# A hybrid conv and retention layer: the heads' norm made chunk by chunk with tokens on partitions, and queries and rotation tables without the token's norm and decay

## The chip, the cores and the metric

One core of one Trainium2 chip runs the whole layer in one launch. The metric is the device time of an execution in microseconds (us). Engines are named as the profile names them: PE (TensorE matmul), PEld (its weight loads), DVE (VectorE), ACT (ScalarE), POOL (GpSimd), SP (SyncE, which issues the DMAs).

## The reference

All arrays are float32, with 1024 tokens of 1024 channels (`D_MODEL`), 8 chunks of 128 tokens, and 4 retention heads of 128 channels.

```python
def rms_norm(x, g, eps=1e-6):
    return x * rsqrt(mean(x * x, -1) + eps) * g

u = rms_norm(x, norm1_g)
z = u @ w_in                       # 3 x 512 conv columns, then q, k, v and gate, 512 each
y_conv = group_rms_norm(cb * causal_dwconv3(cc * ch, conv_w), conv_norm_g, 8)

q, k = rotary(rq), rotary(rk) * 128 ** -0.5
# by head and chunk of 128 tokens, gamma_h = 1 - 2 ** (-5 - h):
scores = q @ k.T * decay           # gamma ** (i - j) where i >= j, else 0
o = scores @ v + (q * xi) @ S      # xi = gamma ** (i + 1)
S = gamma ** 128 * S + (k * zeta).T @ v
y_ret = group_rms_norm(o, ret_norm_g, 4) * silu(rg)

x = x + concat(y_conv, y_ret) @ w_out
x = x + relu(rms_norm(x, norm2_g) @ w_up) ** 2 @ w_down
return rms_norm(x, final_norm_g)
```

## The kernel before, in words

Activations lie with channels on partitions and tokens along the row, so a tile `unit` is 128 channels x 1024 tokens; `hs` are its two halves of 512 tokens. A float32 product is made of three matmuls of rounded float32 parts: each operand is split into a high part (`uh`, `wh`, `U`, made by an ACT copy) and the rest (`ul`, `wl`, made by a subtraction on DVE or POOL). `mm` issues them (before, line 361; 365 in the changed file).

The kernel has these stages, each with its place in the profiled execution:

1. Values (line 323, 6 to 54 us). `v`, with tokens on partitions, is x times its weights, without the token's norm. In the second half of this stage the sum of squares `ssq` is reduced by a matmul with ones (line 333). From it come `R`, the reciprocal norm of every token, laid out along the row on all 128 partitions, and `rtok`, the same with tokens on partitions. The norm of layer input is not applied to x: it is multiplied in later, into what x was projected to.
2. Projections by `tile_in`, two matrix banks (`pm`) of 512 tokens and 48 matmuls each, in four quarters of 12 matmuls. `rot_tiles` makes two such tiles A and B, multiplies both by the cosine and sine tables `ropes` out of PSUM into `ac`, `as_`, `t2`, `t3`, and adds and subtracts these to `q[0]` and `q[1]` (64 partitions each, half on POOL, half on DVE). It runs for queries, then keys, of head pair p = 0, then 1.
3. Retention of a head pair, a generator that is resumed once a quarter, between the matmuls of the tiles of the next stage. A step takes one chunk: scores, turned keys (line 545), and for the chunk before it the product with the values (570), the product with the state (572) and the state's update (578).
4. More projections (`IN_WHOLE`), then the last ones as products of half-sized sums (`pair_in`, seven products for eight), for which `rights` reads x again (`xs`) as soon as the second pair's retention is marked as done.
5. The gate and the convolution (`conv_h`, `conv_b`, `gate`) run beside stages 3 and 4. Then come the output projection (from 375 us), the MLP and the last norm.

PE's order is that of the program. Around it, small planned tasks (`procs`) are asked at every quarter which of them may issue: `background` compares a clock per engine, made of costs per column, with the time of the matmul stream, and where an operation may run on POOL or DVE it takes the one that would end first. So a change of what the tasks issue also moves other tasks' operations from one of the two to the other. Nothing moves an instruction once it is issued: each engine works through its list.

The heads' norm is one of these tasks (`norm`, line 429): for 512 tokens of one head it squares `o` on ACT, splits the square, sums it over the partitions by two matmuls with a matrix of ones (`onesr`, lines 441 and 442), takes the square root on ACT and the reciprocal of 128x512 on DVE, and multiplies `o` by it on POOL or DVE. There are 8 of these, and 8 for the groups of the convolution (`blkr`).

Of the kernel before, what the change touches and what calls it, by code (L numbers as in the profile page):

```python
# [16 lines left out]
P = 128  # L17
# [53 lines left out]
def hybrid_layer(  # L71
# [11 lines left out]
    decay: bass.AP,  # L83
    zeta: bass.AP,
# [139 lines left out]
    onesr = xp.tile([P, P], F32R, name="onesr")  # L224
    dve.tensor_copy(onesr, ones.to_broadcast([P, P]))
# [3 lines left out]
    onesf = xp.tile([P, P], F32, name="onesf")  # L229
    dve.memset(onesf, 1.0)  # L230
# [45 lines left out]
    dec = xp.tile([P, NH, P], F32, name="dec")  # L276
    nc.sync.dma_start(dec, decay)
    zxt = xp.tile([P, NH], F32, name="zxt")
    nc.sync.dma_start(zxt, zeta)
    ropes = [unit(s="rope") for _ in range(6)]  # L280
# [31 lines left out]

    v = [unit(s="v") for _ in range(NC_ // 2)]
    rtok = cp.tile([P, NC_], F32, name="rtok")
    zr = xp.tile([P, NH, NC_], F32, name="zr")
    for half in range(2):
        vb = [bank(pr if half else pm) for _ in range(4)]
        for k in range(KT):
# [11 lines left out]
            if half == 1 and k == 3:  # L330
                for c, sl in ((0, hs[0]), (4, hs[1])):
                    b = bank(pm)
                    nc.tensor.matmul(b, onesf, ssq[:, sl], start=True, stop=True)
                    t = tmp()
                    act.activation(t, b, AF.Sqrt, bias=eps, scale=1.0 / D)
                    dve.reciprocal(R[:, sl], t)
                    t = tmp().rearrange("p (a b) -> p a b", b=P)
                    dve.tensor_mul(
                        t,
                        R[:, sl].rearrange("p (a b) -> p a b", b=P),  # L340
                        ident[:, None, :].to_broadcast([P, 4, P]),
                    )
                    dve.reduce_sum(rtok[:, c : c + 4], t, axis=mybir.AxisListType.X)
# [9 lines left out]
    prepare(2)  # L353

# [169 lines left out]
    def retention(p, q, k):  # L524

        h0 = 2 * p
        S = None
        pend = None
        o = [unit(s="o") for _ in range(2)]
        for c in range(NC_ + 1):  # L530
# [3 lines left out]
            if c < NC_:  # L534
                sl = slice(c * P, (c + 1) * P)
                bs = bank(pr)
                for j in range(2):
                    nc.tensor.matmul(  # L538
# [3 lines left out]
                if c < NC_ - 1:  # L542
                    bt = bank(pr)
                    for j in range(2):
                        nc.tensor.transpose(bt[:, j * P : (j + 1) * P], k[j][:, sl], ident)
# [861 lines left out]
```

## Time and profile before

| what | value |
|---|---|
| median of 3 runs | 1109.75 us (1109.44 to 1110.27) |
| profiled execution | 1111.85 us, of which the span of instructions is 1110.0 us |
| PE busy | 1065.7 us (96%) |
| DVE busy | 926.0 us (83%) |
| POOL busy | 578.1 us (52%) |
| ACT busy | 454.2 us (41%) |
| chain that ended last | PE 77%, DVE 14%, issue 3%, DMA 2%, ACT 2%, POOL 1% |
| mean granted clock of PE | 0.982 of full speed |

The busy share is a mean over stages that have different limits. The table of windows shows which engine is full in which stage; the chain of waits and the order of time around a place show what ends a wait there. Times in a view are microseconds from the start of the span.

### The profile page before, as it was taken

How to read it: one execution, taken by the hardware profiler on the slowest of the kernel's cores; microseconds unless marked ns; L12 is line 12 of the kernel's file. 1: busy time of each engine (PE TensorE's matmuls, PEld its weight loads, DVE VectorE, ACT ScalarE, POOL GpSimd, SP SyncE). 2: the span in 40 equal slices, each digit the busy share in tenths (PEclk: the TensorE clock that was granted, in tenths of full speed). 3: DMA queues.
4: the chain of work that ended last, by engine and by line, in shares of the span. 5: the costliest groups of instructions: out<-in, count | busy, mean ns of one | idle time of the engine just before them, and what ended most of it. 6: DMA issues, size and time to landing. Idle time of an engine off the chain costs nothing.

```text
span 1110.0 us, 13715 instructions
## 1 busy us (share of the span) xinstructions
PE 1065.7 (96%) x4872; PEld 883.4 (80%) x4872; DVE 926.0 (83%) x1171; ACT 454.2 (41%) x817; POOL 578.1 (52%) x393
## 2 busy tenths in 40 slices
PE   7999999998798799989999999999999999999997
PEld 6778888887586588867788888888888888888886
DVE  8786486689999845579999989989989899899945
ACT  8211431456236433354344343433443343434453
POOL 6253234437776323536827629448267286284553
PEclk9999999999899899989999999999999999999998
DMA  7311112130111523032131120221211201200204
GB/s 266 143 57 48 30 39 75 49 142 16 36 46 46 199 86 124 1 100 71 48 96 29 49 86 29 67 58 39 79 37 58 86 29 48 86 20 19 70 9 152
DMA packets 38868, 76.68 MB, mean 69 GB/s; under 512 B 4368, under 2 KB 6416, under 8 KB 38800
## 3 DMA queue, kind: packets, MB, share of 16 engines
q1 hardware_dynamic: 38800, 75.80, 21.1%
q8 instruction: 39, 0.64, 0.2%
q14 instruction: 29, 0.24, 0.1%
HBM read 70.02 MB, written 5.77 MB: 68 GB/s over the span
## 4 chain that ended last, share of the span: by engine, by line
PE 77%; DVE 14%; issue 3%; DMA 2%; ACT 2%; POOL 1%; SPq 0%; DVEq 0%; POOLq 0%; ACTq 0%
PE b L361 49%; PE b L1159 22%; DVE wl L65 3%; PE b L323 2%; DVE U L65 1%; DVE t L65 1%; DVE r L65 1%; DVE z L65 1%; DVE xs L65 1%; DMA wv<-w_v 1%; DVE x L65 1%; DVE cv L65 1%; POOL r L65 1%; PE b L570 1%; PE b L538 1%
## 5 line engine op out<-in xcount | busy, mean ns | idle before, releaser
L65 ACT CAST wh<-r 128x512 fp32r<-128x512 f32 x286 | 176.7, 620 | 385.0 <-PE b L361 204.0
L361 PE MATMUL b<-U,wh 128*128 128x512 f32 x992 | 310.5, 394 | 8.5 <-DVE z L65 3.6
L65 DVE TENSOR_TENSOR wl<-r,wh 128x512 fp32r<-128x512 f32 x257 | 240.2, 937 | 76.1 <-ACT wh L65 75.2
L65 POOL TENSOR_TENSOR r<-r,r 128x512 f32<-128x512 f32 x136 | 210.2, 1548 | 131.6 <-DVE wl L65 79.6
L1159 PE MATMUL b<-V,wh 128*128 128x512 f32 x784 | 242.3, 390 | 1.1 <-POOL V L65 1.1
L361 PEld LDWEIGHTS b<-U,wh 128*128 128x128 f32 x992 | 188.4, 190 | 50.2 <-issue 4.4
L65 DVE TENSOR_TENSOR x<-x,b 128x512 f32<-128x512 f32 (+1 forms) x320 | 198.1, 665 | 28.7 <-PE b L361 28.7
L361 PE MATMUL b<-U,wl 128*128 128x512 f32 x496 | 195.3, 394 | 0.0
L1159 PEld LDWEIGHTS b<-V,wh 128*128 128x128 f32 x784 | 147.0, 188 | 33.1 <-POOL V L65 1.9
L65 POOL TENSOR_TENSOR t<-t,t 128x512 f32<-128x512 f32 x70 | 106.8, 1530 | 101.5 <-ACT t L65 55.4
L1159 PE MATMUL b<-V,wl 128*128 128x512 f32 x392 | 152.5, 389 | 0.0
L361 PE MATMUL b<-uh,wh 128*128 128x512 f32 x320 | 107.0, 399 | 4.3 <-DVE z L65 4.3
L361 PEld LDWEIGHTS b<-U,wl 128*128 128x128 f32 x496 | 94.5, 191 | 19.9
L361 PE MATMUL b<-uh,wl 128*128 128x512 f32 x320 | 105.6, 395 | 1.9 <-DVE wl L65 1.9
L361 PE MATMUL b<-ul,wh 128*128 128x512 f32 x320 | 105.9, 396 | 0.7 <-DVE ul L65 0.7
L65 POOL TENSOR_TENSOR wl<-r,wh 128x512 fp32r<-128x512 f32 x29 | 39.3, 1356 | 98.2 <-ACT wh L65 92.7
L1159 PEld LDWEIGHTS b<-V,wl 128*128 128x128 f32 x392 | 73.6, 188 | 15.2
L65 POOL TENSOR_TENSOR V<-t,V 128x512 fp32r<-128x512 f32 x35 | 49.1, 1402 | 67.2 <-ACT V L65 67.2
L65 DVE TENSOR_TENSOR t<-t,b 128x512 f32<-128x512 f32 x112 | 76.1, 680 | 1.7 <-POOL t L65 1.2
L65 ACT ACTIVATE t<-t 128x512 f32<-128x512 f32 x64 | 40.3, 631 | 84.6 <-DVE t L65 83.9
L361 PEld LDWEIGHTS b<-uh,wh 128*128 128x128 f32 x320 | 60.2, 192 | 17.6 <-issue 4.5
L361 PEld LDWEIGHTS b<-uh,wl 128*128 128x128 f32 x320 | 61.0, 191 | 15.3 <-DVE wl L65 2.4
(155 smaller groups left out, 1505.1 us busy)
## 6 DMA issues: line engine op xcount, KB each, us to landing
r<-w_up_t SPq DMA_DIRECT2D x64, 256.0 KB, 2.6
r<-w_down_t SPq DMA_DIRECT2D x56, 256.0 KB, 2.6
r<-w_in_t SPq DMA_DIRECT2D x48, 256.0 KB, 2.6
xt<-xT SPq DMA_DIRECT2D x16, 256.0 KB, 5.4
xs<-xT SPq DMA_DIRECT2D x8, 512.0 KB, 6.2
r<-w_out_t SPq DMA_DIRECT2D x16, 256.0 KB, 2.6
x<-xT SPq DMA_DIRECT2D x8, 512.0 KB, 8.8
rope<-rope SPq DMA_DIRECT2D x6, 512.0 KB, 6.8
```

The costliest lines, as they stand in the source:

```text
L65: return f(out, *args, **kw)
L323: nc.tensor.matmul(vb[i], a[k][:, tsl], b[k // 2][:, vs], start=(k == 0 and a is uh and b is vh), stop=(k == KT - 1 and a is ul),)
L361: nc.tensor.matmul(b, a[:, k, :], rhs(n, k)[r], start=(start and i == 0), stop=(stop and i == len(ops) - 1),)
L538: nc.tensor.matmul(bs[:, j * P : (j + 1) * P], k[j][:, sl], q[j][:, sl], start=True, stop=True)
L570: nc.tensor.matmul(bo[:, js], vj, sc[:, js], start=True, stop=(S is None))
L1159: nc.tensor.matmul(b, a, r, start=(i == 0), stop=(i == len(ops) - 1))
```

## The change

Four things are changed together.

- `ropes` are only cosine and sine (2 tables for 6); they are not multiplied by `R` any more, and the queries' decay `xi` is not in them. Queries and keys so stay without their token's norm, and queries without their decay. What a key lacks is put in where the scores and the turned keys leave PSUM (`by_key`, `by_state`, a number per token and head, from r squared). What a query lacks is a factor of a whole row of `o`, which the heads' norm divides out; its epsilon is scaled instead (`by_query`).
- `R` and `rtok`: eight one-column matmuls give the sums with tokens on partitions; `R` is made from `rtok` by `spread_norms`, called after the first two tiles (the queries of pair 0): a broadcast copy on DVE, four 128x128 matmuls per half, a copy and a square on ACT.
- Retention gives `o` with tokens on partitions (the operands of lines 570 and 572 change places). Each step then makes the norm of its chunk: two squares on ACT out of PSUM with a sum along the row, three operations on 128x2 (DVE, ACT, DVE), two scaled copies on ACT. One step later two PE transposes and two ACT copies turn it back into `o`. Scores and turned keys now share a bank, as do `bo` and `bk`.
- The 8 norm tasks of the heads are gone, with `onesr`.

```diff
-    onesr = xp.tile([P, P], F32R, name="onesr")
-    dve.tensor_copy(onesr, ones.to_broadcast([P, P]))
...
-    ropes = [unit(s="rope") for _ in range(6)]
+    ropes = [unit(s="rope") for _ in range(2)]
...
             if half == 1 and k == 3:
-                for c, sl in ((0, hs[0]), (4, hs[1])):
-                    b = bank(pm)
-                    nc.tensor.matmul(b, onesf, ssq[:, sl], start=True, stop=True)
-                    t = tmp()
-                    act.activation(t, b, AF.Sqrt, bias=eps, scale=1.0 / D)
-                    dve.reciprocal(R[:, sl], t)
...
-                for i in (0, 1, 4, 5, 2, 3):
-                    pool.tensor_mul(ropes[i], ropes[i], R)
-                R2 = ssq
-                pool.tensor_mul(R2, R, R)
+                b = bank(pm)
+                for c in range(NC_):
+                    nc.tensor.matmul(
+                        b[:, c : c + 1], ssq[:, c * P : (c + 1) * P], ones, start=True, stop=True
+                    )
+                act.activation(ms, b[:, :NC_], AF.Identity, bias=eps, scale=1.0 / D)
+                dve.reciprocal(r2, ms)
+                act.activation(rtok, r2, AF.Sqrt)
                 for h in range(NH):
-                    dve.tensor_scalar_mul(zr[:, h, :], rtok, zxt[:, h : h + 1])
+                    for i, (to, src) in enumerate(((by_key, r2), (by_state, r2), (by_query, ms))):
+                        dve.tensor_scalar_mul(to[:, h, :], src, perhead[:, i, h : h + 1])
...
+    def spread_norms():
+
+        for half, sl in enumerate(hs):
+            r = rtok[:, 4 * half : 4 * half + 4]
+            d = tmp().rearrange("p (a b) -> p a b", b=P)
+            dve.tensor_copy(d, r[:, :, None].to_broadcast([P, 4, P]))
+            b = spread([d[:, j] for j in range(4)])
+            act.copy(R[:, sl], b)
+            act.square(R2[:, sl], R[:, sl])
...
-        for c in range(NC_ + 1):
+        for c in range(NC_ + 2):
...
                 for j in range(2):
-                    nc.tensor.matmul(bo[:, js], vj, sc[:, js], start=True, stop=(S is None))
+                    nc.tensor.matmul(bo[:, js[j]], sc[:, js[j]], vj[j], start=True, stop=(S is None))
...
-                for j in range(2):
-                    act.copy(o[j][:, psl], bo[:, j * P : (j + 1) * P])
...
-                        asked.append((o[j][:, hs[half]], onesr, 1.0 / P, done, clock[act], 0.0))
+                for j in range(2):
+                    act.activation(
+                        on[:, js[j]], bo[:, js[j]], AF.Square, accum_out=m[:, j : j + 1]
+                    )
+                dve.scalar_tensor_tensor(
+                    m, m, 1.0 / P, by_query[:, h0 : h0 + 2, pc], ALU.mult, ALU.add
+                )
+                act.activation(m, m, AF.Sqrt)
+                dve.reciprocal(m, m)
+                for j in range(2):
+                    act.activation(on[:, js[j]], bo[:, js[j]], AF.Copy, scale=m[:, j : j + 1])
+                turn = (pc, on)
+            if turned is not None:
+                pc, on = turned
+                b = bank(pr)
+                for j in range(2):
+                    nc.tensor.transpose(b[:, js[j]], on[:, js[j]], ident)
+                for j in range(2):
+                    act.copy(o[j][:, pc * P : (pc + 1) * P], b[:, js[j]])
...
     for p in range(2):
-        q = rot_tiles(ropes[2 * p], ropes[2 * p + 1])
-        k = rot_tiles(ropes[4], ropes[5])
+        q = rot_tiles(*ropes)
+        if p == 0:
+            spread_norms()
+        k = rot_tiles(*ropes)
```

What this does to the lists of the engines is shown at three places. The first is PE at the end of the first queries' tile B and the start of the keys' tile A, before the change (`uh`, `ul` and `wh`, `wl` are the parts of x and of the weights):

```order
L361 MATMUL b_615<-uh_153,wh_541 128x512
L361 MATMUL b_616<-uh_153,wh_541 128x512
L361 MATMUL b_615<-ul_161,wh_541 128x512
L361 MATMUL b_616<-ul_161,wh_541 128x512
L361 MATMUL b_615<-uh_153,wl_542 128x512
L361 MATMUL b_616<-uh_153,wl_542 128x512
L361 MATMUL b_695<-uh_146,wh_575 128x512
L361 MATMUL b_696<-uh_146,wh_575 128x512
```

The same place on PE with the change; `t_682` and `t_691` are the broadcast copies of `rtok`:

```order
L365 MATMUL b_604<-uh_149,wh_530 128x512
L365 MATMUL b_605<-uh_149,wh_530 128x512
L365 MATMUL b_604<-ul_157,wh_530 128x512
L365 MATMUL b_605<-ul_157,wh_530 128x512
L365 MATMUL b_604<-uh_149,wl_531 128x512
L365 MATMUL b_605<-uh_149,wl_531 128x512
L304 MATMUL b_684<-ident,t_682 128x128 x4
L304 MATMUL b_693<-ident,t_691 128x128 x4
L365 MATMUL b_702<-uh_142,wh_564 128x512
L365 MATMUL b_703<-uh_142,wh_564 128x512
```

Eight matmuls that read DVE's copies stand between the last matmul of the queries and the first of the keys. The second place is DVE's work that follows the queries' tile B, before (`b_615`, `b_616` are its two banks):

```order
L65 TENSOR_TENSOR t_677<-b_615,rope_281 128x512
L65 TENSOR_TENSOR t_678<-b_615,rope_280 128x512
L65 TENSOR_TENSOR q_614<-ac_545,t_677 64x512
L65 TENSOR_TENSOR q_613<-t_678,as_546 64x512
L65 TENSOR_TENSOR t_685<-b_616,rope_281 128x512
L65 TENSOR_TENSOR t_686<-b_616,rope_280 128x512
L65 TENSOR_TENSOR q_614<-ac_545,t_685 64x512
L65 TENSOR_TENSOR q_613<-t_686,as_546 64x512
L65 TENSOR_TENSOR wl_724<-r_603,wh_723 128x512
```

And DVE there with the change:

```order
L65 TENSOR_TENSOR t_666<-b_604,rope_277 128x512
L65 TENSOR_TENSOR t_667<-b_604,rope_276 128x512
L65 TENSOR_TENSOR q_603<-ac_534,t_666 64x512
L65 TENSOR_TENSOR q_602<-t_667,as_535 64x512
L65 TENSOR_TENSOR t_674<-b_605,rope_277 128x512
L65 TENSOR_TENSOR t_675<-b_605,rope_276 128x512
L65 TENSOR_TENSOR q_603<-ac_534,t_674 64x512
L65 TENSOR_TENSOR q_602<-t_675,as_535 64x512
L65 COPY t_682<-rtok 128x512
L65 COPY t_691<-rtok 128x512
L65 TENSOR_TENSOR wl_731<-r_592,wh_730 128x512
```

The two copies stand behind the eight operations that read tile B. The third place is ACT at the end of the second pair's retention, before (`b_2066` is the bank of a norm's sum, `xs` is x read again):

```order
L65 COPY o_1599<-b_1998 128x128
L65 COPY o_1600<-b_1998 128x128
L65 ACTIVATE t_2017<-o_1599 128x512
L65 CAST s_2018<-t_2017 128x512
L65 ACTIVATE t_2019<-o_1600 128x512
L65 CAST s_2020<-t_2019 128x512
L65 CAST wh_2041<-r_1766 128x512
L65 ACTIVATE r_2069<-b_2066,eps 128x512
L65 ACTIVATE xs_2005<-xs_2005,sm 128x1024
```

And ACT there with the change (`h_2095` is a normed chunk, `m_2096` its two norms, `b_2104` and `b_2142` the turned chunks):

```order
L65 ACTIVATE h_2095,m_2096<-b_2090 128x128 x2
L65 ACTIVATE m_2096<-m_2096 128x2
L65 ACTIVATE h_2095<-b_2090,m_2096 128x128 x2
L65 COPY o_1644<-b_2104 128x128
L65 COPY o_1645<-b_2104 128x128
L65 CAST wh_2135<-r_1826 128x512
L65 COPY o_1644<-b_2142 128x128
L65 COPY o_1645<-b_2142 128x128
L65 ACTIVATE xs_2109<-xs_2109,sm 128x1024
```

The squares of 128x512 and the square root that waited for a norm's matmul no longer stand ahead of `xs`.

## Rows read from the trace of the kernel before

**Rows 1.** The page: busy time and share of the span of PE.

```profile
PE 1065.7 (96%) x4872; PEld 883.4 (80%) x4872; DVE 926.0 (83%) x1171; ACT 454.2 (41%) x817; POOL 578.1 (52%) x393
```

**Rows 2.** Windows by stage: PE, PEld, DVE, ACT, POOL busy, clock, DMA share.

```profile
75.00:100.00 25.00, 25.00 (x112) 20.71 (x111) 14.22 (x18) 3.12 (x5) 5.93 (x5) 1.00 0.18 53
100.00:250.00 150.00, 150.00 (x795) 128.57 (x795) 106.77 (x123) 56.87 (x126) 58.91 (x43) 1.00 0.20 66
250.00:375.00 125.00, 104.37 (x418) 82.35 (x416) 120.98 (x111) 57.98 (x94) 87.71 (x57) 0.92 0.14 40
```

**Rows 3.** Timeline of ACT behind tile B: start, duration, operation, idle before it.

```profile
77.37 0.62 ACT L65 CAST wh<-r 128x512 fp32r<-128x512 f32 x1 [4.82 <-PE b L361]
```

**Rows 4.** Timeline of DVE behind the first queries' tile B.

```profile
78.63 1.28 DVE L65 TENSOR_TENSOR t<-b,rope 128x512 f32<-128x512 f32 x2
...
85.58 1.67 DVE L65 TENSOR_TENSOR q<-t,as 64x512 f32<-64x512 f32 x1
87.27 0.69 DVE L65 TENSOR_TENSOR wl<-r,wh 128x512 fp32r<-128x512 f32 x1
```

**Rows 5.** Timeline of DVE before the MLP: the same broadcast copy of norms.

```profile
476.02 0.43 DVE L65 COPY t<-rtok 128x512 f32<-128x512 f32 x1
```

**Rows 6.** Timeline of PE before the MLP: one-column sums (L290) and spreads (L308).

```profile
468.92 0.95 PE L290 MATMUL b<-ones,t 128*128 128x1 f32 x8
...
477.28 1.95 PE L308 MATMUL b<-ident,t 128*128 128x128 f32 x16
478.98 0.71 PE L361 MATMUL b<-U,wh 128*128 128x512 f32 x2
```

**Rows 7.** Windows around waits of PE, columns as in rows 2.

```profile
371.00:378.00 7.00, 3.04 (x7) 2.47 (x8) 6.91 (x10) 3.48 (x7) 1.64 (x1) 0.51 0.51 161
301.00:306.30 5.30, 5.30 (x13) 4.14 (x14) 3.64 (x6) 0.23 (x1) 0.00 (x0) 0.51 0.37 102
```

**Rows 8.** Timeline of PE in the first queries' tile B: a wait for DVE.

```profile
67.52 0.73 PE L361 MATMUL b<-uh,wl 128*128 128x512 f32 x2 [1.93 <-DVE wl L65]
```

**Rows 9.** Chain of waits, first 110 us: start, length, what.

```profile
41.15 1.72 PE b L333 x4
...
108.15 0.22 PE b L545 x2
```

**Rows 10.** Chain of waits at the end of the second retention.

```profile
240.03 5.46 PE b L361 x24
245.49 0.23 PE b L441
245.72 0.25 PE b L442
...
246.58 1.76 ACT xs L65 x2
...
251.37 1.60 DVE xs L65
```

**Rows 11.** Groups of DVE between 250 and 375 us: count, busy, mean ns, idle before.

```profile
L65 DVE RECIPROCAL r<-r 128x512 f32<-128x512 f32 x8 | 26.7, 3343 | 0.7 <-ACT r L65 0.7
L65 DVE TENSOR_TENSOR wl<-r,wh 128x512 fp32r<-128x512 f32 x19 | 20.5, 1081 | 0.1
...
L65 DVE TENSOR_TENSOR s<-t,s 128x512 fp32r<-128x512 f32 x4 | 4.7, 1165 | 0.0
...
L65 DVE TENSOR_TENSOR z<-z,R 128x512 f32<-128x512 f32 x1 | 1.7, 1748 | 0.0
...
L65 DVE TENSOR_TENSOR z<-z,cv 128x512 f32<-128x512 f32 x1 | 0.7, 687 | 0.0
```

**Rows 12.** Groups between 105 and 150 us: turned keys on ACT.

```profile
L65 ACT ACTIVATE h<-b,zr 128x128 f32<-128x128 f32 x14 | 4.4, 367 | 12.3 <-PE b L545 12.3
```

**Rows 13.** Timelines of DVE and POOL, 36 to 105 us: small and large operations at once.

```profile
56.02 8.60 DVE L65 TENSOR_SCALAR zr<-rtok,zxt 128x8 f32<-128x8 f32 x4
52.31 14.59 POOL L65 TENSOR_TENSOR rope<-rope,R 128x1024 f32<-128x1024 f32 x6 [19.65 <-DVE R L65]
```

More of the change, by code (lines that the diff above doesn't have):

```diff
@@ L274, in hybrid_layer @@
     prepare(2)
[L276 to L279, printed above, removed]
-    ropes = [unit(s="rope") for _ in range(6)]
+    causal = xp.tile([P, P], F32, name="causal")
+    nc.sync.dma_start(causal, mask)
+    perhead = xp.tile([P, 3, NH], F32, name="perhead")
+    nc.sync.dma_start(perhead, heads)
+    ropes = [unit(s="rope") for _ in range(2)]
     for i, t in enumerate(ropes):
@@ L314, in hybrid_layer @@
     rtok = cp.tile([P, NC_], F32, name="rtok")
-    zr = xp.tile([P, NH, NC_], F32, name="zr")
+    ms = xp.tile([P, NC_], F32, name="ms")
+    r2 = xp.tile([P, NC_], F32, name="r2")
+    by_key, by_state, by_query = (xp.tile([P, NH, NC_], F32, name=s_) for s_ in ("bk", "bz", "bq"))
     for half in range(2):
@@ L526, in retention @@
         h0 = 2 * p
-        S = None
-        pend = None
+        S = pend = turn = None
         o = [unit(s="o") for _ in range(2)]
-        for c in range(NC_ + 1):
+        js = [slice(j * P, (j + 1) * P) for j in range(2)]
+        for c in range(NC_ + 2):
             yield None
@@ new lines, in retention @@
+                act.activation(m, m, AF.Sqrt)
[8 more added lines that the diff above has]
+                    nc.tensor.transpose(b[:, js[j]], on[:, js[j]], ident)
+                for j in range(2):
+                    act.copy(o[j][:, pc * P : (pc + 1) * P], b[:, js[j]])
+                    if pc % 4 == 3:
+                        o_n[h0 + j, pc // 4] = o[j]
+                        mark(("o", h0 + j, pc // 4), act)
@@ L604, in retention @@
             retention_task[0].ready = max(clock[act], clock[dve])
-        mark(("retention", p), act)
+            if c == NC_:
+                mark(("retention", p), act)
     a_of, cvs = {}, {}
@@ L1317, in _constants @@
     cos, sin = (np.tile(f(ang), (2, 1)) for f in (np.cos, np.sin))
+    rope = np.stack([cos, sin])
     lg = np.log(1.0 - 2.0 ** (-5.0 - np.arange(NH)))
     i = np.arange(P)
-    xi = np.exp(lg[:, None] * (np.arange(T) % P + 1.0)[None])
-    xi = [np.repeat(xi[2 * p : 2 * p + 2], half, axis=0) for p in range(2)]
-    rope = np.stack([cos * xi[0], sin * xi[0], cos * xi[1], sin * xi[1], cos, sin])
+    mask = i[None, :] >= i[:, None]
     scale = P**-0.5
-    decay = np.where(
-        (i[None, :] >= i[:, None])[:, None, :],
-        np.exp(lg[None, :] * (-1.0 - i)[:, None])[:, :, None] * scale,
-        0.0,
-    )
-    zeta = np.exp(lg[None, :] * (P - 1.0 - i)[:, None]) * scale
-    return [np.ascontiguousarray(a, np.float32) for a in (rope, decay, zeta)]
+    heads = np.stack(
+        [
+            np.exp(lg[None] * (-1.0 - i)[:, None]) * scale,
+            np.exp(lg[None] * (P - 1.0 - i)[:, None]) * scale,
+            np.exp(lg[None] * -2.0 * (i + 1.0)[:, None]) * EPS,
+        ],
+        axis=1,
+    )
+    return [np.ascontiguousarray(a, np.float32) for a in (rope, mask, heads)]
 def kernel(x, norm1_g, w_in, conv_w, conv_norm_g, ret_norm_g, w_out, norm2_g, w_up, w_down,
@@ L1376 @@
     )
-    rope, decay, zeta = _constants()
+    rope, mask, heads = _constants()
     arrays = {
@@ L1390 @@
         "rope": rope,
-        "decay": decay,
-        "zeta": zeta,
+        "mask": mask,
+        "heads": heads,
     }
```

74 lines of the change are left out of this document (27 added, 47 removed).

## The prediction, made before the changed kernel was run

> **What bounds the kernel now.** I read the page first. PE is busy for 96% of the span [rows 1], so what counts is where PE stands idle, and whether its list gets longer. The windows by stage say where: from 75 to 250 us PE is never idle and the granted clock is 1.00, though DVE, ACT and POOL have room; from 250 to 375 us it is busy for only 104.4 of 125 us at a mean clock of 0.92, and DVE for 121.0 [rows 2]. So there are two regimes. In the first, through both retentions, any idle time that PE gets is lost for good, and work taken from DVE, ACT or POOL is worth nothing. In the second, DVE is the limit for most of the stretch, and DVE's work and the moment at which it starts count. The change takes work from DVE and POOL and gives some to ACT, and most of the reciprocals that it removes lie in the first regime. Then I compared the lists of the engines, since a stall in the first regime is the one thing to fear.
>
> **Part by part.**
>
> *The first stage.* The two matmuls with ones took 1.72 us of PE [rows 9]; that goes. Eight one-column sums take their place: 0.95 us [rows 6]. The reciprocals of 128x512, the tables' products on POOL and the slow small products (8.60 us for four of 128x8, beside POOL's 14.59 us [rows 13]) leave DVE before 64 us. One wait ended on them: PE stood 1.93 us for a weight part that DVE made too late [rows 8]. With all this gone from DVE and POOL, that wait goes, and I see no other behind it, since the split in question waits only for ACT's copy. Sum of the stage: -1.72 + 0.95 - 1.93 = -2.7 us.
>
> *The spread of the norm.* This is the term that decides. On PE the eight spreads stand right behind the queries' tile B, ahead of the keys' tile A. They read two copies on DVE that stand behind the eight operations which empty tile B, and the first of those needs tile B's last matmuls. In the kernel before, the keys' first matmul followed at once. When tile B ends is seen on ACT: a cast that waits for B's last weights to be free starts at 77.37 [rows 3]. DVE's eight operations ran from 78.63 to 87.27, that is 8.64 us [rows 4]; the copy takes 0.43 [rows 5]; two hand-overs between engines are put at 0.1 us each, an estimate. PE idle: 8.64 + 0.43 + 0.2 = 9.3 us. The first four spreads hide the second copy. All eight cost 1.70 us of PE (477.28 to 478.98 [rows 6]). Everything else that PE could do stands behind them in its list. The bounds of the idle time: if POOL did not hold DVE's 64-partition operations up they would take 0.69 us, as the uncontended subtraction does [rows 4], and the chain 2 x 1.28 + 4 x 0.69 + 0.6 = 5.9 us; if POOL's additional split of a weight, which now stands ahead of its part of the queries, comes between, 1.2 us more than my value (half of 14.59 / 6 [rows 13]), 10.5 us. I take 9.3, since the same eight operations run beside the same four of POOL.
>
> *The clock behind that wait.* After a wait of 6.7 us the granted clock was 0.51 from 371 to 378 us, of which PE worked 3.04; after one of 3.6 us it was 0.51 for 5.30 us of work [rows 7]. That is the lower level, 1.2 for 2.4 GHz, and half of such work is lost: 1.5 to 2.7 us. I take 2.0.
>
> *Retention on PE.* Eight norms with ones go: 0.23 + 0.25 = 0.48 us each [rows 10], -3.8 us. 32 turns come, at 0.11 us (two in 0.22 [rows 9]): +3.5 us. The operands that change places keep their size. Together -0.3 us.
>
> *Retention on ACT and DVE.* Each of the 16 chunk steps adds two squares, a root, two scaled copies, and replaces nothing else but copies; a pass over 128x128 costs ACT 4.4 / 14 = 0.31 us [rows 12], pipelined. With two passes for the keys, two squares, a root (the same 0.31 as a bound), two scaled copies and two turned copies, a step is 9 x 0.31 = 2.8 us of ACT, plus two trips to DVE and back in the middle, where no row shows a price: between the 0.1 us of a hand-over and a whole POOL operation, 1.2 us (half of 14.59 / 6 us for 1024 columns [rows 13]). A step's period on PE is 12 matmuls (half of 5.46 us [rows 10]) and 20 passes of 0.11 us, 4.9 us. So ACT is busy for 3 to 4 us of 4.9, and PE, which reads the normed chunk only in the next step, has over 2 us in hand. I cost it at nothing; the cover is that one step of distance, and without it each step would cost what is late.
>
> That the small operation on 128x2 can be held up by POOL is what the row of the small products shows: 128x8 took 2.15 us apiece while POOL multiplied tables, each as long as one of POOL's operations [rows 13]. The Trainium skill (SBUF — State Buffer, Who interferes with whom) says that VectorE and GpSimd share one pair of ports as an exclusive lock, and that an instruction with two SBUF inputs contends with a reading GpSimd one. By that rule each of the 16 would wait up to a whole POOL operation, and the sum would stay as it is, as 1.2 us is less than the time in hand; it speaks for the third rival below.
>
> *The stretch from 250 to 375 us.* Before, the re-read x came to ACT only after the norm's matmul: 24 matmuls, the norm, a root, then the first scaling at 246.58 and DVE's first difference at 251.37 [rows 10]. With the change ACT reaches it behind the last turned copy, that is after 12 matmuls, two turns and two copies: 246.58 - 240.03 = 6.55 us before, 2.73 + 0.22 + 0.5 = 3.45 now. DVE so starts 3.1 us earlier against PE. What it has to do from there on, counted in the lists up to the last operation before the output projection: one reciprocal less (3.34), four splits of weights less (4 x 1.08), one of a square less (1.2) and a small sum (0.7), together -9.5; and +4 products with R, +3 with the convolution, one difference of x and one split more, nine of 0.69 to 1.75 us, at 1.2 us each +10.8. So the planner gives back to DVE what the norms leave: +1.3 us. POOL has five operations less there, some 7 us of its 87.7 [rows 2], and as an uncontended split takes 0.69 and the mean one 1.08 [rows 4, 11], about a third of that comes back to DVE: -2.3 us. Sum: -3.1 + 1.3 - 2.3 = -4.1 us. Bounds: +4 if the nine all take 1.75 us and POOL gives nothing, -9 if they take 0.69 and DVE is the limit throughout.
>
> *Behind 375 us* the lists are the same, and PE is the limit.
>
> **Sum.** -2.7 + 9.3 + 1.7 + 2.0 - 0.3 - 4.1 = +5.9 us. On the profiled execution (span 1110.0 and 1.85 around it, 1111.85) that is 1117.8. That execution lies 2.1 above the median of the runs, 1109.75; put on the median the forecast is 1115.6 us, slower by 0.5%.
>
> **Rivals.**
>
> 1. *The stretch gives all of it back.* The wait in front of the keys is paid, but DVE, which starts with less behind it, ends the stretch 9 us or more earlier, and PE, which waits for it 20.6 us there [rows 2], follows. For it: those 20.6 us and the clock of 0.92. Against it: the count of DVE's work, which is nearly the same. -2.7 + 9.3 + 1.7 + 2.0 - 0.3 - 9 = +1 us: 1110.8.
> 2. *DVE is no longer the limit between 250 and 375 us.* This ends on the other side. One mechanism: with less of POOL in its way DVE keeps ahead of the matmuls, and PE's idle 20.6 us goes, and with it some of the 10 us that a clock of 0.92 is worth over 125 us. It decides from the point at which the stretch shrinks by more than 10 us; with 15 us the time is 1109.75 + 10 - 15 = 1104.8. Against it: the six reciprocals of the convolution stay, 20 of the 26.7 us [rows 11]. The same side comes out if the wait for the spread is not there at all (1104.3), for which nothing in the lists speaks.
> 3. *The chunk's chain is late.* Square, sum, root, reciprocal and scaling cross between ACT and DVE four times; if POOL's lock or ACT's other copies make it longer than a step, PE stands at the turns, in the regime where all is lost. At 0.5 us in each of 16 steps +8 us: 1123.6. Against it: over 2 us in hand.
>
> **How the numbers follow.** Forecast 0.62, with its own range 1112.5 to 1119; rival 1: 0.14; rival 2 and the missing wait: 0.10; rival 3: 0.14. The range 1109.5 to 1122.5 holds the forecast, rival 1 and the near half of rival 3, and leaves out rival 2 and the far half. A measurement of this kernel can tell about 0.2% (2.2 us) from no change. Slower: forecast, rival 3 and a little of rival 1, 0.78; within: most of rival 1, 0.12; faster: 0.10.
>
> **What would show it.** In the profile after: one gap of PE of 8 to 10 us at about 75 us, ended by DVE's copy at the spread, with a lower granted clock behind it; no wait in the queries' tile B; no gaps in the two retentions; DVE over 0.9 busy again in the 125 us that follow the second one, and the output projection starting some 6 us later than the 375 us of now. The forecast is wrong if that gap is under 5 us, if PE waits at the turns, or if the stretch behind the second retention is shorter by more than 9 us.

## The result, and the profile after

The changed kernel takes 1114.2 us (median of 5 runs, 1113.53 to 1115.23), the kernel before 1110.23 in the same session (5 runs, 1109.44 to 1110.35): a ratio of 1.0038, 95% interval 1.0025 to 1.0051. It is slower by 0.4%; 1115.6 had been forecast. One run of experiment 3 took 6104 us and is left out of its times below.

The profiled executions stand closer together: 1113.53 us against 1111.85 (spans 1111.7 and 1110.0). That of before lies 1.6 above the median beside it, that of after 0.7 below. So the traces have to explain +1.7, the runs +4.0, and the difference of 2.3 is between executions (experiment 12).

The page of the kernel after, its line of busy times (of before: [rows 1]):

```profile
PE 1064.8 (96%) x4916; PEld 885.2 (80%) x4916; DVE 872.1 (78%) x1207; ACT 462.1 (42%) x909; POOL 542.7 (49%) x377
```

The windows of after, with the columns of [rows 2] (PE, PEld, DVE, ACT, POOL, granted clock, DMA); the last one is the eight spreads by themselves:

```profile
75.00:100.00 25.00, 16.04 (x72) 13.53 (x72) 11.04 (x13) 4.30 (x7) 8.04 (x6) 0.80 0.08 22
100.00:250.00 150.00, 150.00 (x809) 129.12 (x808) 81.34 (x157) 58.45 (x201) 44.43 (x33) 1.00 0.21 67
250.00:375.00 125.00, 109.16 (x465) 86.32 (x464) 118.18 (x115) 62.57 (x107) 79.37 (x54) 0.98 0.14 43
...
84.39:87.82 3.43, 3.43 (x16) 3.43 (x17) 0.28 (x1) 1.21 (x2) 0.00 (x0) 0.50 0.00 0
```

DVE is busy 54 us less than before, and the kernel is slower. In the first 25 us shown PE now stands idle for 9; through the retentions it is again never idle; in the third window it works 4.8 us more than before.

The timeline of PE in after at the spread: the last matmuls of the queries' tile B, the spreads, the keys' first matmul.

```profile
74.81 0.61 PE L365 MATMUL b<-uh,wl 128*128 128x512 f32 x2
84.39 3.72 PE L304 MATMUL b<-ident,t 128*128 128x128 f32 x16 [8.96 <-DVE t L65]
87.82 0.73 PE L365 MATMUL b<-uh,wh 128*128 128x512 f32 x2
```

The timeline of DVE in after, over the same wait (of before: [rows 4]): eight operations on tile B, then the copy that PE waits for.

```profile
75.31 1.29 DVE L65 TENSOR_TENSOR t<-b,rope 128x512 f32<-128x512 f32 x2 [7.39 <-PE b L365]
76.63 0.90 DVE L65 TENSOR_TENSOR q<-ac,t 64x512 f32<-64x512 f32 x1
77.56 1.64 DVE L65 TENSOR_TENSOR q<-t,as 64x512 f32<-64x512 f32 x1
...
83.90 0.76 DVE L65 COPY t<-rtok 128x512 f32<-128x512 f32 x2
```

This is the wait that was forecast. After it the granted clock is 0.50, the lower level, and the spreads take 3.43 us.

Behind the second retention, the timelines of ACT and DVE in after where the re-read x arrives (of before: [rows 10]):

```profile
253.78 0.43 ACT L65 COPY o<-b 128x128 f32<-128x128 f32 x2
254.10 4.28 ACT L65 ACTIVATE xs<-xs,sm 128x1024 f32<-128x1024 f32 x4
```

```profile
253.33 1.29 DVE L65 TENSOR_TENSOR z<-b,R 128x512 f32<-128x512 f32 x2 [1.49 <-PE b L365]
254.54 1.17 DVE L65 TENSOR_TENSOR z<-z,cv 128x512 f32<-128x512 f32 x1
255.63 1.78 DVE L65 TENSOR_TENSOR xs<-xs 128x512 f32<-128x512 f32 x1
```

And the same spot in before, where a reciprocal of the heads' norm stood ahead of x on DVE:

```profile
246.99 3.34 DVE L65 RECIPROCAL r<-r 128x512 f32<-128x512 f32 x1
250.25 1.00 DVE L65 TENSOR_TENSOR xs<-xs 128x512 f32<-128x512 f32 x1
```

The keys' first matmul is PE's next one behind the queries' tile B; in the timeline of before it starts at 77.62:

```profile
77.62 0.62 PE L361 MATMUL b<-uh,wh 128*128 128x512 f32 x2
```

The last product of the second retention with the state ends at 240.03 in before and 250.55 in after, 162.4 and 162.7 us behind that matmul. From there DVE needs 10.2 us to get to x in before (250.25) and 5.1 in after (255.63). The output projection starts at 374.96 and 375.91: 134.9 us behind the end of that product before, 125.4 after. So the two traces add up in this way:

| piece | before to after, us |
|---|---|
| first matmul (6.31, then 5.79) | -0.5 |
| from there to the end of the queries' tile B | -1.7 |
| wait at the spread | +9.0 |
| spreads, at clock 0.50 | +3.4 |
| retentions | +0.3 |
| last product with the state to the output projection | -9.6 |
| from the output projection on | +0.8 |
| sum | +1.7 |

A delay of 12.4 us in front of the keys, and 9.6 us given back behind the retentions. The windows of that stretch, from the end of the last product with the state to the output projection, first in before, then in after:

```profile
240.03:374.96 134.93, 114.30 (x462) 90.46 (x460) 129.06 (x116) 65.25 (x105) 91.30 (x59) 0.92 0.13 39
```

```profile
250.55:375.91 125.36, 108.61 (x461) 85.80 (x459) 119.06 (x117) 63.20 (x108) 79.37 (x54) 0.98 0.15 43
```

PE's idle time falls by 3.9 us (20.6 to 16.8), the time it works by 5.7, with a mean granted clock of 0.98 for 0.92; DVE is busy for 10.0 us less. Three explanations fit the 9.6. **Theory A**: these are two independent effects; the spread costs its 12 us in any case, and the new norm saves its 9.6 in any case, so the loss can be had back without losing the gain. **Rival B**: the stretch behind the retentions, where PE waits for other engines anyway, takes up whatever delay it is given; then the norm saves little, and removing the wait gains little. **Rival C**: the higher clock gives the time back, whatever DVE does.

### The profile page after: what moved, and what is told of

Read it like the earlier page. It is cut to its first block, busy times and chain, and to the rows that moved or that the text cites. A ratio compares the mean times of both kernels' runs of the same rounds, so it can differ in the third digit from the quotient of the medians.

```text
span 1111.7 us, 13918 instructions
## 1 busy us (share of the span) xinstructions
PE 1064.8 (96%) x4916; PEld 885.2 (80%) x4916; DVE 872.1 (78%) x1207; ACT 462.1 (42%) x909; POOL 542.7 (49%) x377
## 4 chain that ended last, share of the span: by engine, by line
PE 75%; DVE 12%; issue 2%; ACT 2%; POOL 1%; DVEq 0%; POOLq 0%; ACTq 0%
PE b L365 49%; PE b L1173 22%; DVE wl L65 2%; DVE z L65 2%; DVE r L65 1%; DVE U L65 1%; DVE x L65 1%; DVE t L65 1%; PE b L571 1%; PE b L542 1%; PE b L573 1%; PE b L579 1%; DVE xs L65 1%; DVE cv L65 1%; PE b L304 1%
## 5 line engine op out<-in xcount | busy, mean ns | idle before, releaser
L65 DVE TENSOR_TENSOR wl<-r,wh 128x512 fp32r<-128x512 f32 x249 | 227.5, 916 | 112.2 <-ACT wh L65 111.4
L65 POOL TENSOR_TENSOR r<-r,r 128x512 f32<-128x512 f32 x136 | 207.9, 1531 | 131.2 <-DVE wl L65 79.5
L65 POOL TENSOR_TENSOR wl<-r,wh 128x512 fp32r<-128x512 f32 x37 | 49.8, 1350 | 166.4 <-ACT wh L65 150.3
L365 PEld LDWEIGHTS b<-ul,wh 128*128 128x128 f32 x320 | 60.3, 189 | 15.7 <-DVE ul L65 2.9
```

The source lines that it names most:

```text
L65: return f(out, *args, **kw)
L365: nc.tensor.matmul(b, a[:, k, :], rhs(n, k)[r], start=(start and i == 0), stop=(stop and i == len(ops) - 1),)
```

## The experiments

Experiments 1 to 4, 5 to 8, and 9 to 11 each share their runs of before (medians 1110.42, 1109.88 and 1110.08 us). Where kernels of different groups are compared below, their ratios to before give the same differences within 0.4 us.

**1. The spread moved up.** The copies follow the small products on DVE, the spreads follow the values on PE; behind that all lists are as in the changed kernel.

```diff
+    spread_norms()            # right behind the values' loop, banks from pm
     prepare(2)
...
         q = rot_tiles(*ropes)
-        if p == 0:
-            spread_norms()
```

> The changed kernel with the spread of the tokens' norm moved: its copies stand on DVE behind the small products at 45 us, its matmuls on PE right behind the values' matmuls at 53.5 us. Behind that the lists of all engines are those of the changed kernel. Theory A (PE's wait of 8.97 us at the spread and the lower clock behind it are a loss by themselves, and the retention's new norm saves its share whether they are there or not): the wait goes and the spreads take 1.7 instead of 3.43 us, 1114.2 - 8.97 - 1.7 = 1103.5 us, and the output projection starts some 10.7 us before 375.9. Rival B (the stretch behind the second retention takes up whatever PE lost before it, since PE waits there for other engines anyway): that stretch gets longer by most of 10 us, the output projection starts at 374 to 375 us as in both kernels, 1112 to 1114 us.

Measured: 1102.79 us (1102.59 to 1104.12; 0.9935 of before, 0.9924 to 0.9947). The timeline of PE: no wait, and half the time for the spreads.

```profile
53.90 1.95 PE L304 MATMUL b<-ident,t 128*128 128x128 f32 x16
55.60 0.71 PE L366 MATMUL b<-uh,wh 128*128 128x512 f32 x2
...
365.49 0.77 PE L366 MATMUL b<-yh,wh 128*128 128x512 f32 x1 [6.06 <-ACT z L65]
```

53.90 to 55.60 is 1.70 us for the same eight spreads, at a granted clock of 1.00. The output projection starts 10.4 us earlier than in after: the wait and the clock are pure loss, and nothing of the norm's gain depends on them. A held, B did not.

**2. The kernel before with the same spreads, of no use.**

```diff
         q = rot_tiles(ropes[2 * p], ropes[2 * p + 1])
+        if p == 0:
+            for half in range(2):
+                r = rtok[:, 4 * half : 4 * half + 4]
+                d = tmp().rearrange("p (a b) -> p a b", b=P)
+                dve.tensor_copy(d, r[:, :, None].to_broadcast([P, 4, P]))
+                b = spread([d[:, j] for j in range(4)])
+                t = tmp()
+                act.copy(t, b)
+                act.square(t, t)
         k = rot_tiles(ropes[4], ropes[5])
```

> The kernel before, with two broadcast copies of the tokens' norm on DVE behind the first queries' tile B, eight spreads on PE ahead of the keys' tile A and two copies and squares on ACT, whose results nobody uses; all else as it was. Theory A: PE loses the wait (9 to 10 us), the spreads (1.7) and the clock (1.7), nothing is given back, 1110.2 + 12.5 = 1122.7 us. Rival B (the stretch takes the delay up by itself): the output projection starts at 375 to 378 us instead of 375, 1111 to 1114 us. Between the two, what is given back without the new norm is read from the stretch.

Measured: 1124.39 us (1124.22 to 1124.93; 1.0129, 1.0116 to 1.0142), +14.0; between the traced spans it is 12.4 (1122.4 and 1110.0). The timeline of PE at the spread and at the output projection:

```profile
85.17 3.78 PE L308 MATMUL b<-ident,t 128*128 128x128 f32 x16 [9.88 <-DVE t L65]
88.60 1.20 PE L361 MATMUL b<-uh,wh 128*128 128x512 f32 x2
...
386.42 0.76 PE L361 MATMUL b<-yh,wh 128*128 128x512 f32 x1 [6.64 <-DVE z L65]
```

From the keys' first matmul to the output projection are 297.8 us; in before they are 297.3 (77.62 to 374.96). So with the old norm the delay is not given back: the stretch moves as a whole. The same trace decides Rival C. The window of the stretch:

```profile
252.41:386.42 134.01, 109.52 (x461) 86.17 (x460) 129.46 (x116) 65.23 (x105) 91.29 (x59) 0.98 0.13 40
```

PE has the clock of 0.98 here, and works 4.8 us less than in before; but it then waits 24.5 us for 20.6, and the stretch is only 0.9 us shorter. What stayed is DVE's work, 129.5 us for 129.1. C did not hold.

**3 and 9. The new norm alone.** Retention as in after, first stage as in before (two tables with the token's norm, no spread).

```diff
-                b = bank(pm)
-                for c in range(NC_):
-                    nc.tensor.matmul(
-                        b[:, c : c + 1], ssq[:, c * P : (c + 1) * P], ones, start=True, stop=True
...
+                    nc.tensor.matmul(b, onesf, ssq[:, sl], start=True, stop=True)
...
+                for i in range(2):
+                    pool.tensor_mul(ropes[i], ropes[i], R)
```

> The retention of the changed kernel (norm with tokens on partitions, turned back), with the first stage of the kernel before: matmuls with ones of 128x512, wide reciprocals, POOL multiplies two tables with the tokens' norm, no spread. Theory A: the norm saves what the changed kernel gave back, so 1110.2 - 7 = 1103 us, with the output projection starting some 6 to 7 us before 375. Rival B: without a delay to take up the stretch has nothing to give, 1109 to 1110 us. The prediction's own term for it (-0.3 on PE, -4.1 in the stretch) gives 1105.8.

Measured: 1100.92 us (median of five runs, 1100.59 to 1102.68; 0.9922, 0.991 to 0.9934), 9.5 below the median of before, 8.7 by the ratio. The trace is that of experiment 9, the same kernel.

> The kernel with the new norm alone once more, for its trace: time 1101.8 us as before; a wait of some 1.9 us in the first queries' tile B, none at the keys; from the keys' first matmul to the output projection 288 us as in the changed kernel, where the kernel before had 297.6.

Measured: 1101.52 us (one run). The output projection starts at 363.76, 287.8 us behind the keys' first matmul (the queries' first, 54.20, and 96 matmuls of 0.2267); in after it is 288.1 (87.82 to 375.91). The expected wait in tile B was not there: PE has no wait of over 0.6 us between its first matmul and 264 us. Why is seen on DVE and POOL:

```profile
56.99 1.53 DVE L65 TENSOR_SCALAR bk<-rtok,perhead 128x8 f32<-128x8 f32 x1
58.44 1.94 DVE L65 TENSOR_SCALAR bz<-rtok,perhead 128x8 f32<-128x8 f32 x1
60.29 1.33 DVE L65 TENSOR_SCALAR bq<-ones,perhead 128x8 f32<-128x8 f32 x1
61.53 0.22 DVE L65 TENSOR_SCALAR bk<-rtok,perhead 128x8 f32<-128x8 f32 x1
```

```profile
53.28 5.21 POOL L65 TENSOR_TENSOR rope<-rope,R 128x1024 f32<-128x1024 f32 x2 [20.07 <-DVE R L65]
58.46 1.89 POOL L65 TENSOR_TENSOR ssq<-R 128x1024 f32<-128x1024 f32 x1
60.31 1.28 POOL L65 TENSOR_TENSOR wl<-r,wh 128x512 fp32r<-128x512 f32 x1
```

A product of 128x8 takes 0.22 us alone and 1.3 to 1.9 as long as POOL is at work. With two tables instead of six POOL is done at 61.6, and DVE's first weight split comes in time.

**4. The new first stage and the spread alone**, with the retention of before.

```diff
-        q = rot_tiles(ropes[2 * p], ropes[2 * p + 1])
-        k = rot_tiles(ropes[4], ropes[5])
+        q = rot_tiles(*ropes)
+        if p == 0:
+            spread_norms()
+        k = rot_tiles(*ropes)
```

> The first stage of the changed kernel (one-column sums, small products, two tables without norm and decay, the spread behind the first queries) with the retention of the kernel before, whose norm goes through squares, matmuls with ones and wide reciprocals. The queries' decay and norm are left out there, so that the constant under the root weighs otherwise. Theory A: the wait (8.97), the spreads (3.43), the wait that goes (-1.93) and the sums (+0.4) come to +10.9, nothing given back: 1121 us. Rival B: the stretch takes most of it up, 1111 to 1114 us.

Measured: 1123.7 us (1122.53 to 1124.45; 1.0121, 1.0106 to 1.0136), +13.3, more than either theory; between the traced spans it is 11.4, near the 10.9 expected, and experiment 12 says what may lie between the two. PE waits 8.95 us at the spread; its timeline at the keys' first matmul and at the output projection:

```profile
88.49 1.03 PE L364 MATMUL b<-uh,wh 128*128 128x512 f32 x2
...
386.26 0.77 PE L364 MATMUL b<-yh,wh 128*128 128x512 f32 x1 [6.65 <-DVE z L65]
```

Again 297.8 us from the keys to the output projection. The two parts add up: -9.5 + 13.3 = +3.8, where the whole change measured +4.0.

**5. No spread at all.** The norm is made wide by matmuls with ones and reciprocals, as before; the tables stay bare, and the products per head are made from `rtok`.

```diff
+                    dve.reduce_sum(rtok[:, c : c + 4], t, axis=mybir.AxisListType.X)
+                    act.square(ssq[:, sl], R[:, sl])
+                dve.tensor_mul(r2, rtok, rtok)
+                dve.reciprocal(ms, r2)
```

> The changed kernel with the tokens' norm made wide again by matmuls with ones (1.31 us of PE) and reciprocals of 128x512, the products per head made small from it, tables left alone, and no spread at all; the lists behind the first stage are those of the changed kernel. Theory: PE loses neither the one-column sums (1.70) nor the spreads (1.70 where they were moved up), and with no table product on POOL the small products take 0.2 us apiece instead of 2.15, so the wait of 1.93 us for a weight part stays away: 1102.8 - 2.1 = 1100.7 us. Rival: the wide reciprocals alone make DVE late for that weight part, the wait is back, 1102.6 us.

Measured: 1101.21 us (1100.82 to 1101.67; 0.9922, 0.9908 to 0.9936), 13 us below the changed kernel and level with the new norm alone (1100.92 and 1101.52). PE does not wait in tile B. It is worth 1.6 against the kernel with the spread moved up, for 2.1 expected.

The next four ask where the 9.6 us come from. Each adds work of no use to the kernel of experiment 1, meant for the stretch behind the second retention (in experiment 8 only a part of it lies there); all other instructions keep their order.

**6. Two reciprocals back on DVE.**

```diff
             act.activation(t, t, AF.Copy, scale=sm[:, G1 + k : G1 + k + 1])
+        if j in (1, 2):
+            nc.vector.reciprocal(ropes[j - 1][:, lo_], R[:, lo_])
```

> The kernel with the spread moved up (1102.8 us), with two reciprocals of 128x512 of no use on DVE, one ahead of the first difference of the re-read x and one two operations behind it; all lists are else unchanged. Theory A (behind the second retention DVE's time, from the moment it gets to x up to the output projection, sets the end): 2 x 3.34 = 6.7 us come back, less what DVE's waits in the stretch take up (under 3 us): 1107 to 1109.5 us, output projection starting 4 to 6.7 us later than 365.5. Rival B (PE's own pace there and POOL set it; the norm saved its time in another way): 0 to 1.5 us.

Measured: 1109.06 us (1108.08 to 1109.79), +6.3 of 6.7 put in: 0.9993 of before, 0.9984 to 1.0002, so two reciprocals cost nearly the whole gain. The timelines of PE at a norm's matmul of the convolution, first of experiment 1, then of this kernel:

```profile
267.00 0.50 PE L447 MATMUL b<-s,blkr 128*128 128x512 f32 x1 [0.62 <-DVE s L65]
```

```profile
268.29 0.79 PE L447 MATMUL b<-s,blkr 128*128 128x512 f32 x1 [5.53 <-DVE s L65]
...
370.93 0.77 PE L366 MATMUL b<-yh,wh 128*128 128x512 f32 x1 [6.06 <-ACT z L65]
```

Most of the time comes back as a wait of PE for DVE, at 263 us, behind the two reciprocals (245 to 254 us).

**7. ACT later at x.**

```diff
+        if j == 1:
+            for _ in range(3):
+                nc.scalar.square(ropes[0], R)
         for k, t in ((j, a), (4 + j, b)):
```

> The kernel with the spread moved up (1102.8 us), with three squares of 128x1024 of no use on ACT ahead of the first scaling of the re-read x behind the second retention, some 3.3 us; all else unchanged. It puts back the later start of x that the norm's matmul and root had caused (3.0 us). Theory A (the moment at which DVE gets to x counts in full): 1105.5 to 1106 us. Rival B (DVE has other work or waits there anyway, and the work that the norm took from DVE is all that counts): 0 to 1 us.

Measured: 1106.36 us (1105.15 to 1106.47; 0.9965, 0.9953 to 0.9978), +3.6 for 3.3: the moment at which DVE gets to x counts in full.

**8. Five products more on POOL.**

```diff
     for f in IN_WHOLE[1]:
+        nc.gpsimd.tensor_mul(ropes[0][:, hs[0]], R[:, hs[0]], R[:, hs[0]])
         whole(f)
```

> The kernel with the spread moved up (1102.8 us), with five products of 128x512 of no use on POOL, one ahead of each of the five whole tiles behind the second retention; all else unchanged. The prediction took 2.3 us for five POOL operations less in that stretch. Theory A (DVE is held up by about a third of POOL's time): +2 to +3, 1105 us. Rival B (DVE's and POOL's operations do not hold each other up enough to show, or the time is taken up by waits): within 0.5 us of 1102.8. More than 4 us would show that POOL is itself the bound there.

Measured: 1105.06 us (1104.78 to 1105.63; 0.9958, 0.9944 to 0.9971), +2.3, the size that the prediction had for five operations of POOL in the stretch. But the edit put only two of the five there. The timeline of POOL:

```profile
202.69 1.37 POOL L767 TENSOR_TENSOR rope<-R 128x512 f32<-128x512 f32 x1
...
246.74 1.49 POOL L767 TENSOR_TENSOR rope<-R 128x512 f32<-128x512 f32 x1
...
261.46 1.48 POOL L767 TENSOR_TENSOR rope<-R 128x512 f32<-128x512 f32 x1
```

Three ran at 202.69, 209.60 and 228.64, in the second retention, whose last turns are at 243.34. So the agreement of the +2.3 is no evidence for that price. In the traces 1.1 of the 2.3 lies between the last turns and the output projection (243.34 to 367.04, against 242.86 to 365.49), 0.1 ahead of the keys, 0.4 in the retentions and 0.7 behind the output projection, where nothing was changed. The 1.1 us are a third of the 3.0 that the two products take on POOL, from one trace of each kernel. The Trainium skill (SBUF — State Buffer, Who interferes with whom) says that a DVE instruction with two inputs in SBUF contends with a POOL instruction that reads SBUF, and that the order of issue decides which of them blocks the other. The two groups of DVE in this stretch that read only x agree in direction: from experiment 1 to this one their means go from 1.22 to 1.36 us and from 1.04 to 1.14.

**10. All three at once** (the diffs of 6, 7 and 8 together, each with a place of its own to write to).

> The kernel with the spread moved up, with all three of the foregoing put back at once: three squares on ACT ahead of x, two reciprocals of 128x512 on DVE, five products of 128x512 on POOL. Theory A1 (one chain, each counts in full): 6.3 + 3.6 + 2.3 = 12.2 us on 1102.8, 1115 us. Theory A2 (ACT's delay and the first reciprocal lie beside each other, as in the kernel before, where x was scaled by 248.7 while DVE stood in a reciprocal from 246.99 to 250.25): one of the two, 3.3 us, is hidden by the other: 1111.5 to 1112 us, which is near what the norm gave back in all (9.5 us).

Measured: 1109.64 us (1108.29 to 1111.05; 0.9995, 0.9987 to 1.0004), +6.9, less than either sum. The timelines of ACT and DVE:

```profile
242.20 3.27 ACT L744 ACTIVATE rope<-R 128x1024 f32<-128x1024 f32 x3
...
246.20 4.28 ACT L65 ACTIVATE xs<-xs,sm 128x1024 f32<-128x1024 f32 x4
```

```profile
244.64 3.35 DVE L749 RECIPROCAL rope<-R 128x512 f32<-128x512 f32 x1
247.90 1.25 DVE L65 TENSOR_TENSOR xs<-xs 128x512 f32<-128x512 f32 x1
```

As A2 says, ACT's delay lies beside the first reciprocal: x is scaled while DVE still divides. That explains 3.3 us. That POOL's 2.3 hardly show any more is not explained; here too only two of its five products lie in the stretch.

**11. More on POOL.**

```diff
-    pool = Engine(nc.gpsimd, 2.4, now, clock)
+    pool = Engine(nc.gpsimd, 2.1, now, clock)
```

> The kernel without spreads (1101.2 us) with POOL's planned cost per column at 2.1 instead of 2.4, by which four or five small operations of the stretch behind the second retention go from DVE to POOL. Theory A: each takes 0.7 us from DVE and holds it up by some 0.46 us through POOL: 0 to -1.2 us, 1100 to 1101.2. Rival: an operation that stands on POOL comes too late for the matmul that needs it, 1102 to 1104 us.

Measured: 1104.37 us (1103.16 to 1105.15; 0.9947, 0.9934 to 0.9959), 3.2 more than with 2.4. Theory A fell; the time lies 0.4 above the rival's range, and the rival's mechanism is not shown. From the end of the last product with the state to the output projection are 128.0 us (238.46 to 366.47) for 125.2 in experiment 5 (238.71 to 363.95). DVE is busy there for 117.9 us, 0.9 less, and POOL for 84.3, 4.0 more. PE's waits add up to nearly the same, 16.6 and 16.4 us, and none of them ends on POOL; what grew is the time of the same matmuls, 111.4 us for 108.8, at a mean granted clock of 0.96 for 0.97. So a smaller sum on DVE was no gain here; which operation came later than before stays open.

**12. The kernel before once more.** In its first trace PE waited 1.93 us in tile B [rows 8]; in experiment 2, with the same first stage, it did not.

> The kernel before, unchanged, for a second trace. In its first trace PE stood 1.93 us in the first queries' tile B, as DVE's first weight split took 2.92 us beside POOL's table product; in the trace of the same first stage with spreads behind it that split took 0.6 us, came in time, and PE did not wait. Theory A (whether the split gets in ahead of POOL's next product differs from execution to execution, and the first trace, 1.6 us above the median of its runs, holds a wait that most runs lack): no wait there, span about 1108.2, 1110 us. Rival B (the wait is always there, the other trace is the exception): a wait of 1.9 us again.

Measured: 1112.48 us, span 1110.7; a second run beside it took 1111.80. The first split of a weight behind the products per head, on DVE, in experiment 2 and then in this run, with PE's wait:

```profile
64.22 0.68 DVE L65 TENSOR_TENSOR wl<-r,wh 128x512 fp32r<-128x512 f32 x1
```

```profile
64.39 2.93 DVE L65 TENSOR_TENSOR wl<-r,wh 128x512 fp32r<-128x512 f32 x1
```

```profile
67.38 0.74 PE L361 MATMUL b<-uh,wl 128*128 128x512 f32 x2 [1.94 <-DVE wl L65]
```

Theory A fell in this trace: the wait is there again. (The granted clock differs: behind the wait it was 1.00 from 67.5 to 72.0 us in the first trace and 0.63 from 67.4 to 72.0 in this one, and the queries take 25.7 us here for 24.0.) In two traces of three the split was held up beside POOL's table product, in one it got in between. How often it is so in the runs without a trace stays open. That experiments 2 and 4 lie 14.0 and 13.3 us above the median of before, but only 12.4 and 11.4 above its trace, speaks for runs of before that mostly lack the wait, and is no proof. Those of before reach from 1107.65 to 1114.25 us in one session (15 runs), those of experiment 5 from 1100.82 to 1101.67 (4 runs).

## Why the prediction was right, and where its terms were off

The time and the decisive step were right: PE's list got a wait in the regime where nothing is given back, 8.96 us for 9.3 forecast, ended by the copy that was named, and it makes the kernel slower, with the spreads and their clock (experiments 1, 2 and 4). The stretch behind the retentions was not: it is 9.6 us shorter, over the 9 that the prediction named as a sign of being wrong, and the output projection starts 0.95 us later, not some 6. By its steps:

- *First stage*, -2.7: measured -1.7. The wait in tile B went, as said. The sums were mis-sized: the row of eight that was used [rows 6] holds four sums in two passes each, so eight sums are sixteen instructions and take 1.70 us, not 0.95:

```profile
40.78 1.84 PE L333 MATMUL b<-ones,ssq 128*128 128x1 f32 x16
```

- *Wait at the spread*, +9.3: +8.96. POOL's weight split came between (75.71 to 76.98), but it did not cost the 1.2 us of the upper bound: DVE's eight operations took 8.59 us for 8.64, and DVE began 0.1 us before tile B's last matmul ended. The cast at 77.37, read as the end of tile B, waits for the last use of the high part only; tile B ended at 77.78. The sum does not use it. The two hand-overs, put at 0.1 us each with no row for them, are small: 0.06 us from the end of the first copy (84.33) to the first spread (84.39).
- *Spreads and clock*, +1.7 and +2.0: +3.43 together, twice the 1.70 of experiment 1.
- *Retention*, -0.3 on PE and nothing for ACT and DVE: +0.3, with no gap. The third rival did not come: the chain of squares, root, reciprocal and scaling takes 1.9 us from the first square to the last scaled copy (250.59 to 252.50 for the last chunk), in a step of 5.
- *Stretch behind the retentions*, -4.1: -9.6, beyond the range that was given for it (+4 to -9; with the prices named there the upper end adds up to +3). Two of its terms were mis-sized. The first is "DVE so starts 3.1 us earlier against PE". The start was worked out on ACT, whose part was right: from the product with the state to x 6.55 us before, 3.55 now. But in before DVE was not waiting for ACT; a reciprocal of the norm stood ahead of x until 250.25 (251.37 [rows 10] is where the chain passes to DVE, not the start of DVE's first difference). So DVE started 5.1 us earlier. The second is the count of DVE's work, +1.3. From x to the output projection DVE took 120.1 us for 124.6 (255.63 to 375.77, 250.25 to 374.82), -4.4 where +1.3 and -2.3 had been summed. The numbers of operations were right, the prices not: by the sums of their groups the nine that came took 9.0 us for 10.8 (the products with R 0.89 each, those with the convolution 1.19, by the means below), and those that went took 11.0 for 9.5 (the splits of weights alone 5.3, 20.5 to 15.2, for 4.3). That is -2.0 for +1.3. The operations that stayed took 2.5 us less, for the 2.3 that were put down to POOL; that POOL is the cause is not shown. The groups of DVE in after, from x to the output projection (of before: [rows 11]):

```profile
L65 DVE RECIPROCAL r<-r 128x512 f32<-128x512 f32 x6 | 20.1, 3342 | 1.3 <-ACT r L65 1.3
...
L65 DVE TENSOR_TENSOR wl<-r,wh 128x512 fp32r<-128x512 f32 x15 | 15.2, 1011 | 1.5 <-ACT wh L65 1.5
...
L65 DVE TENSOR_TENSOR z<-z,cv 128x512 f32<-128x512 f32 x5 | 6.0, 1191 | 0.1
L65 DVE TENSOR_TENSOR z<-z,R 128x512 f32<-128x512 f32 x5 | 4.5, 894 | 0.0
```

- Experiments 6 and 7 show that DVE's work and its start count there (reciprocals nearly in full, the start in full); experiment 8 has only two products of POOL in the stretch, and 1.1 us for them. Put back together they return 6.5 us in the trace (from the last turns to the output projection 129.2 against 122.6 us), of 9.6. The other 3 us were not tried; the splits and squares that went are the likely place.
- *Rival 1*, "the stretch gives all of it back", had the right size for that stretch (9.6 for its 9) and for the traces (+1.7 for its +1), and with "DVE, which starts with less behind it" the right cause as far as experiments 6 and 7 show it. What the prediction held against it, a count of DVE's work that is nearly the same, is what failed. That the time still came out near the forecast is in part luck. Between the traces +5.9 was forecast and +1.7 measured, 4.2 off: -5.5 in the stretch, +1.0 in the first stage and +0.3 in small terms. In the runs the error is only 1.4, since the traced executions differ from their medians by 2.3 in all, and the median of before rose by 0.5 with its last two runs.

## What to carry to other kernels

Where an engine is never idle, ask of every instruction put into its list what the list of its producer holds ahead: here two copies of 0.4 us cost 12 us, because they stood behind eight operations that need the very matmuls before them, while their own input had been ready for 39 us (44.45 to 83.90). A change that measures "slightly slower" may be two large effects of opposite sign: undo each part by itself before dropping it, as the norm was worth some 9 us and only the place of its helper was wrong. And work out the start of an engine from its own list as well as from its input; the later of the two counts.

## What the runs showed of the hardware

- A square on ACT that also sums along the row brings a second instruction. The timeline of ACT in after:

```profile
250.59 0.28 ACT L65 ACTIVATE h<-b 128x128 f32<-128x128 f32 x1 [1.04 <-PE b L573]
250.76 0.19 ACT L65 ACTIVATION_READ_ACCUMULATOR h<-b 128x1 f32 x1
```

- At the lower clock level work takes twice as long: the same 16 passes took 3.43 us at a granted 0.50, behind a wait of 9 us, and 1.70 at 1.00. A wait does not always bring it: behind the same wait in the queries' tile B, 1.93 and 1.94 us in two executions of before, the granted clock was 1.00 in the one and 0.63 over the next 4.6 us in the other.
- A higher clock of PE is worth little where DVE is full: 4.8 us less work of PE made the stretch 0.9 us shorter (experiment 2).
- A DVE operation of 128x8 takes 0.22 us or up to 1.94, by whether POOL is at work; a split of 128x512 took 0.68 (experiment 2) or 2.93 (experiment 12) at the same place of the same first stage.
